# Moving the first attention head's weighted sum by one period, and turning the residual to tokens in squares of 32 and a trip through DRAM

## The chip, the cores and the metric

The kernel runs on one core of one Trainium2 chip. The metric is the device time of one execution in microseconds. A core has five engines with their own instruction streams: PE (TensorE, matrix products), DVE (VectorE), ACT (ScalarE), POOL (GpSimd) and SP (SyncE, which here only starts DMAs). They meet through semaphores. PE writes its products to PSUM, which has eight banks of 128 partitions x 2 KB; DVE and ACT read them from there.

## The reference

One layer of a hybrid block over 512 tokens and 16 meta tokens (T = 528), width 1024, all in fp32:

```python
h = h + 0.5 * swiglu(rmsnorm(h, ffn1_norm), w_gate, w_up, w_down)        # FFN 1, d_ff 2816
h = h + hybrid_mixer(rmsnorm(h, mix_norm), pos, k_top, w_in, w_ret_out, w_att_out, w_mix_out)
h = h + 0.5 * swiglu(rmsnorm(h, ffn2_norm), w_gate, w_up, w_down)        # FFN 2
y = rmsnorm(h, final_norm)                                               # the 512 real tokens

# in hybrid_mixer
merged = sigmoid(g_ret) * yr + sigmoid(g_att) * ya                       # retention and attention
return merged @ w_mix_out
```

`ya` is an attention of 8 heads of 128 over the keys that an index score selects (at most 128 of them here, and the 16 meta keys), with rotary positions: per head, scores of queries and keys, a softmax, and the sum of the values weighted by it.

## The kernel before, in words

*Layout and precision.* Activations are kept transposed: features on the 128 partitions, the 512 tokens along the free dimension, eight blocks of features. Every fp32 operand of a product is split in two parts, hi and lo (`split`: ACT copies hi, line L117, DVE subtracts, L118). A product is three matmuls per block, hi x hi, hi x lo and lo x hi (`mm3`, L157). Weights come in 1 MB or 512 KB loads on SP's queue (`raw`, two buffers) and are split into `whi` and `wlo` (three buffers each). A `Cols` object hands out one weight column block of 128 after the other; a product of one column with 512 tokens is 24 matmuls.

*Order.* PE's instructions stand in the order in which the program issues them; a few stretches also fix ACT and DVE. Elsewhere a scheduler orders the other engines' instructions. On every queue an instruction that waits holds up what stands behind it.

*PSUM in the mixer.* Two tiles of two banks (`mm_tile`) and four of one bank (`sm_tile`), each kind handed out in rotation. A tile is free again when its last reader is through.

*Attention heads* (loop over `h` in `range(AH)`, L2073 on). In head h's period PE does: the scores of head h (`psS`, 15 matmuls, L1970; DVE adds the bias and takes the maximum, L1973; ACT exponentiates, L1976); the query and key projections of head h+1 (`psaq`, `psak`), then rotated by ACT, DVE and POOL (L1292 to L1296) and split into `aq` and `ak`, which the next scores need; the weighted sum of head h-1 (`psao`); and a column of a gate projection (`psgate` or `psga`). For the weighted sum the probabilities have to lie with keys on the partitions. For heads 1 to 6 DVE transposes them in squares of 32 (`turn`, L1996), POOL writes them to DRAM (`pd`, L2000), SP reads them back in order (`land`, L2006), and `weigh_turned` multiplies them in the next period. For heads 0 and 7 PE transposes them (`transpose_p`, `psPT`, four blocks in four `sm` tiles), ACT and DVE split them from PSUM into `pth` and `ptl`, and `weigh_v` (`weighted`, L1537, L1538) multiplies them in the same period, behind one gate column for head 0 and head 7.

*The mixer's output* (L2133 on). Eight columns `psmo`, 24 matmuls each. Per column: ACT loads the residual `hc` from DRAM (`hd`); DVE adds the product to it (L2164); ACT scales it and splits it with DVE into `xh` and `xl` for FFN 2; ACT squares it, and POOL (DVE for the last column) adds up the squares (`ssum`, L296). The residual is also needed with tokens on the partitions, for the end of the kernel: `to_tokens` transposes two columns at a time on PE (eight transposes `psht`, L2149), and ACT copies them to `hTok` (four tiles of 128 tokens x 1024, L2151). The groups stand behind `psmo` of columns 2, 4 and 6, and, as `last_tokens`, behind the first gate product `psg` of FFN 2. Behind that comes the norm (`rstd_folded`): the sums of squares are folded (ACT L215, L218, DVE L217, L220), PE adds over partitions (`psn`, L225), DVE and POOL make the reciprocal root (L249, `rcol` L251, L276 to L282), PE spreads it (`psn`, L265).

*FFN 2* ends in products with tokens on the partitions. A first part of them is added into `hTok` in two bursts of four DVE additions (`add_sums`, L2241, 128x512 each), later parts likewise, and the final norm reads `hTok` (L2296).

Of the kernel before, what the change touches and what calls it, by code (L numbers as in the profile page):

```python
# [11 lines left out]
F32 = mybir.dt.float32  # L12
F32R = mybir.dt.float32r
AF = mybir.ActivationFunctionType
ALU = mybir.AluOpType
# [66 lines left out]
def kernel(ctx: ExitStack, tc: tile.TileContext, x, meta, g1, wg1, wu1, wd1, gm,  # L82
# [226 lines left out]
    gd = dpool.tile([2 * KD, P, S], F32, name="gd")  # L309

    pd = dpool.tile([2, S, 4, P], F32, name="pd")

    def gap(p, n):

# [1595 lines left out]
    with pool("ao") as ao:  # L1910
        vo = [ao.tile([P, AH, S], F32R, tag=f"vo{i}", name="vo") for i in range(2)]
        ao_parts = [(vo[0][:, c, :], vo[1][:, c, :]) for c in range(AH)]
        with pool("at") as at:
# [163 lines left out]
            for h in range(AH):  # L2077
                more = h + 1 < AH
                if h:
                    scores(q, k)  # L2080
                if more:
                    q, k = proj_q(w if h == 0 else None), proj_k()
                else:
                    wide_gate(sm_tile("psga"))
                    wide_gate()
                if pend is not None:
                    weigh_turned(h - 1, pend, vs[h - 1])
                    pend = None
                if h == 0:
                    with tc.manual_schedule(engines=BUSY):  # L2090
                        vs += split_values(raw, [v[:, 4:, :] for v in vo])
                    vrs.close()
                    crp = crs.enter_context(pool("cross", 1, side="right"))
                    cross = crp.tile([P, 16, 4, 32], F32, tag="cross", name="cross")
                    for j in range(3):
                        nc.gpsimd.memset(cross[:, 4 * j + 5 :, j, :], 0.0)
                if 0 < h and more:
                    turn(h)
                    wide_gate(sm_tile("psga"))
                    turned(h)  # L2100
                    pend = turned_parts()
                else:
                    pt = transpose_p()
                    wide_gate()
                    weigh_v(h, pt, vs[h])
                if h == 4:
                    place_tails(5)

        crs.close()

# [25 lines left out]
    hpool = ctx.enter_context(pool("hpool", 1))  # L2136
    hTok = [hpool.tile([P, D], F32, tag=f"hTok{b}", name=f"hTok{b}") for b in range(4)]
    ssum3 = hpool.tile([P, S], F32, tag="ssum3", name="ssum3")
    R3 = hpool.tile([P, S], F32, tag="R3", name="R3")
    new_ident2(hpool)  # L2140
    s2 = Sevens(S, S, wg2, wu2)
    s2.sums = ctx.enter_context(pool("sums2", 1))
    with pool("om") as ou:
        tp.update(pool=ou, bufs=3)
        def to_tokens(blocks):
            for c, hc in blocks:
                ps = sm_tile("psht")
                for b in range(4):
                    nc.tensor.transpose(ps[:, b * P : (b + 1) * P], hc[:, b * P : (b + 1) * P], ident)  # L2149
                for b in range(4):  # L2150
                    nc.scalar.activation(hTok[b][:, c * P : (c + 1) * P], ps[:, b * P : (b + 1) * P], AF.Copy)  # L2151

        cols = Cols(w_mo, 0, KD)
        pend = []
        for c in range(KD):
            hc = ou.tile([P, S], F32, tag="hc", name="hc", bufs=4)
            nc.scalar.dma_start(hc, hd[c])
            w = cols.next()
            ps = sm_tile("psmo")
            mm3([(ps, slice(0, S))], w, lambda k: mg[k], KD)  # L2160
            if len(pend) == 2:
                to_tokens(pend)
                pend = []
            nc.vector.tensor_tensor(hc, ps, hc, ALU.add)  # L2164
            h, l = new_x(c)
            if c % 4 == 0:
                s2.new_scaled()
            xc = s2.xn[c // 4][:, c % 4, :]
            nc.scalar.activation(xc, hc, AF.Identity, scale=gains[:, 2, c : c + 1])
            split(xc, h[:, :S], l[:, :S])  # L2170
            add_square(hc, ssum3, c == 0, ou, S, eng=(nc.gpsimd, nc.vector)[c == KD - 1])
            pend.append((c, hc))
        last_tokens = lambda a=pend: to_tokens(a)
        RS = slice(0, S)


        norm = rstd_folded(ssum3, D, R3, ou, lambda: mm_tile("psn"), lambda: sm_tile("psn"))
        raw0 = load_w(wg2[:, 0 : 2 * P], KD, 2 * P)
        ps0 = [sm_tile("psg") for _ in range(2)]
        for i in range(2):  # L2180
            w = split_w(raw0[:, :, i * P : (i + 1) * P])
            mm3([(ps0[i], RS)], w, xs, KD)
            if i == 0:
                last_tokens()
                next(norm)
        raw0 = load_w(wu2[:, 0 : 2 * P], KD, 2 * P)
        w = split_w(raw0[:, :, :P])
        for _ in norm:
            pass
    mgs.close()  # L2190
    accs.close()
    sel.close()
# [4 lines left out]
    with pool("hid2") as hidp, pool("f2ps", 8, PSUM) as f2ps, ExitStack() as later:  # L2197
# [39 lines left out]
            st.append(s2.gate_of(pss[1], ts[:, 1, :], R))  # L2237
            psus.append(tile_of(w, "psu"))

        def add_sums(b, cs, ps):  # L2240
            nc.vector.scalar_tensor_tensor(hTok[b][:, cs], ps, 0.5, hTok[b][:, cs], ALU.mult, ALU.add)  # L2241

        def products(parts, b, k, w, j, first, last):

# [6 lines left out]
        def down(f0, nf, n, taken_by):  # L2251


            d = {}
            steps = []
            for at in range(n):
                c, k0 = divmod(at * 2, nf)

                def pre(at=at, c=c, k0=k0):
                    if at % 2 == 0:  # L2260
                        d["raw"] = wpool.tile([P, 2048], F32, tag="raw", name="raw", bufs=2).rearrange("p (k c) -> p k c", k=4)
                    d[at] = d["raw"][:, at % 2 * 2 : at % 2 * 2 + 2]
                    rows = slice((f0 + k0) * P, (f0 + k0 + 2) * P)
                    nc.sync.dma_start(d[at], wd2[rows, c * S : (c + 1) * S].rearrange("(k p) c -> p k c", p=P))

                def run(w, lower, c=c, k0=k0):
                    if k0 == 0:
                        d["ps"] = [[(s2.bank("psd"), slice(0, S))] for _ in range(4)]
                        if f0 == groups[-1] and c == 1:
                            d["ps"][3] = [(s2.bank("psd")[:, : S // 2], slice(i * S // 2, (i + 1) * S // 2)) for i in range(2)]  # L2270
                    for b in range(4):
                        for k in range(k0, k0 + 2):
                            products(d["ps"][b], b, f0 + k, w, k - k0, k == 0, k == nf - 1)
                        if b == 1:
                            lower()
                            s2.catch_up()
                    if k0 == nf - 2:
                        for b in range(4):
                            add_sums(b, slice(c * S, (c + 1) * S), d["ps"][b][0][0])
                            taken_by(b, c)  # L2280
                    s2.next_sum4()

                steps.append((pre, lambda at=at: d[at], run))
            return steps, d
# [6 lines left out]
        def finish(b, c):  # L2291

            p, sums, hg = fin["p"], fin["sums"], fin["hg"]
            cs = slice(c * 512, (c + 1) * 512)
            junk = p.tile([P, 512], F32, tag="junk", name="junk", bufs=2)
            nc.scalar.activation(junk, hTok[b][:, cs], AF.Square, accum_out=sums[:, b, c : c + 1])  # L2296
            nc.vector.tensor_tensor(hg[b][:, cs], hTok[b][:, cs], fin["gfb"][:, cs], ALU.mult)
            if c == 0:
                nc.vector.tensor_scalar(sums[:, b, 0:1], sums[:, b, 0:1], 1.0 / D, EPS, ALU.mult, ALU.add)
                return None  # L2300
            ms = p.tile([P, 2], F32, tag="fms", name="fms", bufs=4)
            nc.vector.tensor_scalar(ms[:, 0:1], sums[:, b, 1:2], 1.0 / D, sums[:, b, 0:1], ALU.mult, ALU.add)
            nc.gpsimd.tensor_tensor(ms[:, 1:2], ms[:, 0:1], mhalf[:, 0:1], ALU.pow)
            return ms[:, 1:2]
# [54 lines left out]
        with tc.manual_schedule(engines=BUSY):  # L2359
# [5 lines left out]
                    products([part], 3, f0 + k, ws[k // 2 - 1], k % 2, False, k == 5)  # L2365
            ready = None
            for b in range(3):
                add_sums(b, slice(S, D), last["ps"][b][0][0])
                r = finish(b, 1)
                if ready:  # L2370
                    leave(*ready)
                ready = (b, r)
            sums, hg = fin["sums"], fin["hg"]
            for i, (ps, q) in enumerate(last["ps"][3]):
                cs = slice(S + q.start, S + q.stop)
                add_sums(3, cs, ps)
                junk = fp.tile([P, 512], F32, tag="junk", name="junk", bufs=2)
                nc.scalar.activation(junk[:, q], hTok[3][:, cs], AF.Square, accum_out=sums[:, 3, 1 + i : 2 + i])
                nc.vector.tensor_tensor(hg[3][:, cs], hTok[3][:, cs], fin["gfb"][:, cs], ALU.mult)
                if i == 0:  # L2380
                    nc.vector.tensor_scalar(sums[:, 3, 0:1], sums[:, 3, 1:2], 1.0 / D, sums[:, 3, 0:1], ALU.mult, ALU.add)
            leave(*ready)
# [31 lines left out]
```

## Time and profile before

| | |
|---|---|
| median of 3 runs | 1512.89 us (1512.02 to 1515.25) |
| the profiled execution | 1512.66 us, span 1510.8 us, mean granted clock 0.997 |
| PE busy | 1498.6 us, 99% of the span |
| DVE busy | 1113.5 us, 74% |
| ACT busy | 729.9 us, 48% |
| POOL busy | 122.2 us, 8% |
| mean DMA rate | 122 GB/s |

Head 0's sum begins at 910 us of the span and head 7's ends at 1068; the attention's output projection follows, the mixer's output fills 1111 to 1158, and FFN 2 the rest. A row of the timeline is: start, length, engine, line, operation, output<-inputs, shape, count, and in brackets how long the engine was idle before it and what ended that. The chain that ended last is the path that set the end; a row of it is start, length, engine, tile and line, count. PE's rows overlap a little, since matmuls are pipelined.

### The profile page before, as it was taken

What the parts mean: (1) busy time and instruction counts of PE and PEld (TensorE: products, weight loads), DVE (VectorE), ACT (ScalarE), POOL (GpSimd) and SP (SyncE); (2) the same over time, 40 slices, a digit from 0 to 9 for tenths busy, and PEclk for the clock granted to TensorE, in tenths of its full rate; (3) what the DMA queues carried; (4) which work ended last, traced back from release to release, by engine and by line L of the source; (5) the groups of instructions that cost most, each with busy time, mean ns of one, the idle gap of its engine ahead of it and who ended that gap; (6) DMA issues with size and microseconds to landing.
All of it is one profiled execution on the core that took longest, in us unless ns stands there. A gap on an engine that the chain in (4) does not pass through costs nothing.

```text
span 1510.8 us, 23879 instructions
## 1 busy us (share of the span) xinstructions
PE 1498.6 (99%) x9664; PEld 1361.2 (90%) x9664; DVE 1113.5 (74%) x1740; ACT 729.9 (48%) x1134; POOL 122.2 (8%) x169
## 2 busy tenths in 40 slices
PE   9999999999999999999999998999999999999998
PEld 8999999999988888888898887988888899899996
DVE  4988585786786768678978887787455888586675
ACT  5555263454354444443333356677345445254453
POOL 1000000002111120000000132331001000000000
PEclk9999999999999999999999999999999999999999
DMA  5232323226544444232322244566443223233232
GB/s 170 64 121 87 116 92 112 86 96 200 205 149 168 167 146 158 87 122 72 117 93 87 95 130 134 154 189 193 147 135 124 84 84 110 86 112 112 84 117 93
DMA packets 161918, 184.90 MB, mean 122 GB/s; under 512 B 12048, under 2 KB 130344, under 8 KB 161168
## 3 DMA queue, kind: packets, MB, share of 16 engines
q1 hardware_dynamic: 151056, 156.70, 32.3%
q0 software_dynamic: 5920, 17.68, 3.5%
q10 hardware_dynamic: 4832, 9.00, 1.7%
q8 instruction: 76, 1.25, 0.3%
q14 instruction: 34, 0.28, 0.1%
HBM read 161.05 MB, written 22.30 MB: 121 GB/s over the span
## 4 chain that ended last, share of the span: by engine, by line
PE 97%; DVE 1%; ACT 1%; issue 1%; DMA 0%; POOL 0%; POOLq 0%; DVEq 0%; ACTq 0%
PE psqX L157 14%; PE psd L157 8%; PE psd L2249 8%; PE psqY L157 7%; PE psrg L157 6%; PE psro L157 6%; PE psvX L1181 4%; PE psqZ L157 3%; PE psrk L157 3%; PE psu L157 3%; PE psrq L157 3%; PE psga L157 3%; PE psat L157 3%; PE psmo L157 3%; PE psak L157 3%; PE psaq L157 3%
## 5 line engine op out<-in xcount | busy, mean ns | idle before, releaser
L329 ACT ACTIVATE whi<-raw 128x1024 fp32r<-128x1024 f32 (+2 forms) x184 | 169.5, 924 | 129.0 <-PE psd L157 37.5
L330 DVE TENSOR_TENSOR wlo<-raw,whi 128x1024 fp32r<-128x1024 f32 (+2 forms) x184 | 198.6, 1083 | 40.6 <-ACT whi L329 40.5
L157 PE MATMUL psqX<-th,whi 128*128 128x264 f32 (+1 forms) x432 | 122.3, 283 | 0.0
L157 PE MATMUL psqX<-tl,whi 128*128 128x264 f32 (+1 forms) x432 | 122.3, 283 | 0.0
L157 PE MATMUL psqX<-th,wlo 128*128 128x264 f32 (+1 forms) x432 | 122.2, 283 | 0.0
L329 ACT ACTIVATE whi<-wsum 128x1024 fp32r<-128x1024 f32 x72 | 76.3, 1060 | 70.7 <-PE psd L2249 22.0
L117 ACT ACTIVATE whi<-raw 128x1024 fp32r<-128x1024 f32 (+1 forms) x60 | 62.2, 1043 | 86.0 <-PE psat L157 26.6
L330 DVE TENSOR_TENSOR wlo<-wsum,whi 128x1024 fp32r<-128x1024 f32 x72 | 87.8, 1221 | 12.5 <-ACT whi L329 12.5
L118 DVE TENSOR_TENSOR wlo<-raw,whi 128x1024 fp32r<-128x1024 f32 (+1 forms) x60 | 73.6, 1228 | 28.3 <-ACT whi L117 27.4
L157 PEld LDWEIGHTS psqX<-th,whi 128*128 128x128 f32 x432 | 82.1, 190 | 0.1
L157 PEld LDWEIGHTS psqX<-tl,whi 128*128 128x128 f32 x432 | 82.0, 190 | 0.0
L157 PEld LDWEIGHTS psqX<-th,wlo 128*128 128x128 f32 x432 | 82.0, 190 | 0.0
L157 PE MATMUL psro<-vo,whi 128*128 128x512 f32 x256 | 78.7, 389 | 0.0
L157 PE MATMUL psd<-hl,whi 128*128 128x264 f32 x352 | 71.3, 284 | 0.0
L157 PE MATMUL psd<-hh,wlo 128*128 128x264 f32 x352 | 70.8, 283 | 0.0
L157 PE MATMUL psd<-hh,whi 128*128 128x264 f32 x352 | 70.7, 282 | 0.0
L2249 PE MATMUL psd<-wlo,hh 128*128 128x512 f32 (+1 forms) x182 | 69.2, 382 | 0.0
L2249 PE MATMUL psd<-whi,hh 128*128 128x512 f32 (+1 forms) x182 | 69.2, 382 | 0.0
L2249 PE MATMUL psd<-whi,hl 128*128 128x512 f32 (+1 forms) x182 | 69.2, 382 | 0.0
L157 PEld LDWEIGHTS psro<-vo,whi 128*128 128x128 f32 x256 | 48.0, 188 | 10.1 <-DVE vo L330 0.2
L157 PEld LDWEIGHTS psd<-hh,wlo 128*128 128x128 f32 x352 | 54.5, 188 | 0.0
L157 PEld LDWEIGHTS psd<-hh,whi 128*128 128x128 f32 x352 | 54.2, 188 | 0.0
(476 smaller groups left out, 4540.8 us busy)
## 6 DMA issues: line engine op xcount, KB each, us to landing
raw<-in_ffn_w_up_dram SPq DMA_DIRECT2D x22, 1024.0 KB, 5.0
raw<-in_ffn_w_gate_dram SPq DMA_DIRECT2D x21, 1024.0 KB, 5.0
raw<-in_w_in_dram SPq DMA_DIRECT2D x18, 1024.0 KB, 5.0
raw<-in_w_in_dram SPq DMA_DIRECT2D x33, 512.0 KB, 3.8
raw<-in_ffn_w_down_dram SPq DMA_DIRECT2D x24, 512.0 KB, 4.4
w<-in_w_in_dram SPq DMA_DIRECT2D x24, 512.0 KB, 6.1
raw<-in_ffn_w_down_dram SPq DMA_DIRECT2D x12, 768.0 KB, 4.4
raw<-in_w_ret_out_dram SPq DMA_DIRECT2D x8, 1024.0 KB, 4.8
```

The source lines that it names most:

```text
L117: nc.scalar.activation(hi, src, AF.Copy)
L118: eng.tensor_tensor(lo, src, hi.bitcast(F32), ALU.subtract)
L157: nc.tensor.matmul(o, a[:, k, :], b[:, sl], start=first and k == 0 and i == 0, stop=last and k == nk - 1 and i == 2, skip_group_check=onto)
L329: nc.scalar.activation(hi, src, AF.Copy)
L330: return lambda: nc.vector.tensor_tensor(lo, src, hi.bitcast(F32), ALU.subtract)
L1181: nc.tensor.matmul(d[bank_][t], a, b[:, k, :], start=not onto and j + k + m == 0, stop=j + k == 3 and m == 2, skip_group_check=onto)
L2249: nc.tensor.matmul(ps, a[:, bs], m[:, j, cs], start=first and i == 0, stop=last and i == 2)
```

## The change

1. `weigh_v` of head 0 is issued in head 1's period, behind the projections for head 2, at the place where `weigh_turned` stands for the later heads. `pend` then always holds the parts of the head before; the sum of head 7 follows the loop.
2. `to_tokens` no longer uses PE, PSUM and ACT. Per column DVE transposes two halves of `hc` (128x256) in squares of 32 into `hTok`, which serves as staging. After every fourth column POOL writes the staged tiles to a DRAM tensor `hx` (eight DMAs of 128 KB each time, in runs of 512 bytes), and after the norm POOL reads `hx` back into `hTok` (four DMAs of 512 KB).
3. In `hx`, and so in `hTok`, the 512 features of a half stand in another order: the group of 32 within a block comes ahead of the block. The first addition of FFN 2 to each half of each tile (`in_order`) puts them right: four DVE operations of 128 elements a partition each, into a free tile (`spare`, or a half that has been read). `home` remembers where each half now is. Later additions are as before.

```diff
+    hx = dpool.tile([S, 2, 4, P], F32, name="hx")
...
                 if pend is not None:
-                    weigh_turned(h - 1, pend, vs[h - 1])
-                    pend = None
+                    (weigh_turned, weigh_v)[h == 1](h - 1, pend, vs[h - 1])
...
                 else:
-                    pt = transpose_p()
+                    pend = transpose_p()
                     wide_gate()
-                    weigh_v(h, pt, vs[h])
                 if h == 4:
                     place_tails(5)
+            weigh_v(AH - 1, pend, vs[AH - 1])
...
-        def to_tokens(blocks):
-            for c, hc in blocks:
-                ps = sm_tile("psht")
-                for b in range(4):
-                    nc.tensor.transpose(ps[:, b * P : (b + 1) * P], hc[:, b * P : (b + 1) * P], ident)
-                for b in range(4):
-                    nc.scalar.activation(hTok[b][:, c * P : (c + 1) * P], ps[:, b * P : (b + 1) * P], AF.Copy)
+        def to_tokens(c, hc):
+            half, j = divmod(c, 4)
+            for g in range(2):
+                t = hTok[2 * half + g]
+                nc.vector.transpose(t.rearrange("p (b j i) -> p b j i", j=4, i=32)[:, :, j, :],
+                                    hc[:, g * 2 * P : (g + 1) * 2 * P].rearrange("p (b i) -> p b i", i=32))
+                if j == 3:
+                    for a in range(4):
+                        nc.gpsimd.dma_start(hx[g * 2 * P : (g + 1) * 2 * P, half, a].rearrange("(b q) e -> q b e", q=32),
+                                            t[32 * a : 32 * a + 32].rearrange("p (b e) -> p b e", e=P))
...
-            if len(pend) == 2:
-                to_tokens(pend)
-                pend = []
...
-            pend.append((c, hc))
-        last_tokens = lambda a=pend: to_tokens(a)
+            if c < KD - 1:
+                to_tokens(c, hc)
...
             if i == 0:
-                last_tokens()
                 next(norm)
+                to_tokens(KD - 1, hc)
...
         for _ in norm:
             pass
+        for b in range(4):
+            nc.gpsimd.dma_start(hTok[b], hx[b * P : (b + 1) * P].rearrange("t h a e -> t (h a e)"))
...
-        def add_sums(b, cs, ps):
-            nc.vector.scalar_tensor_tensor(hTok[b][:, cs], ps, 0.5, hTok[b][:, cs], ALU.mult, ALU.add)
+        home, free = {}, [spare]
+
+        def in_order(b, c, ps):
+            t = hTok[b][:, c * S : (c + 1) * S]
+            o = home[b, c] = free.pop()
+            for a in range(4):
+                view = [x.rearrange("p (j a i) -> p a j i", a=4, i=32)[:, a] for x in (o, ps)]
+                nc.vector.scalar_tensor_tensor(view[0], view[1], 0.5, t[:, a * P : (a + 1) * P].rearrange("p (j i) -> p j i", i=32),
+                                               ALU.mult, ALU.add)
+            free.append(t)
+
+        def add_sums(b, c, ps, q=slice(0, S)):
+            if (b, c) not in home:
+                return in_order(b, c, ps)
+            t = home[b, c][:, q]
+            nc.vector.scalar_tensor_tensor(t, ps, 0.5, t, ALU.mult, ALU.add)
```

The remaining lines of the diff replace `hTok[b][:, cs]` by `home[b, c]` where the final norm reads it.

More of the change, by code (lines that the diff above doesn't have):

```diff
@@ L2138 @@
     ssum3 = hpool.tile([P, S], F32, tag="ssum3", name="ssum3")
+    spare = hpool.tile([P, S], F32, tag="spare", name="spare")
     R3 = hpool.tile([P, S], F32, tag="R3", name="R3")
@@ L2160 @@
             mm3([(ps, slice(0, S))], w, lambda k: mg[k], KD)
-            if len(pend) == 2:
-                to_tokens(pend)
-                pend = []
             nc.vector.tensor_tensor(hc, ps, hc, ALU.add)
@@ L2278, in run @@
                         for b in range(4):
-                            add_sums(b, slice(c * S, (c + 1) * S), d["ps"][b][0][0])
+                            add_sums(b, c, d["ps"][b][0][0])
                             taken_by(b, c)
@@ L2295, in finish @@
             junk = p.tile([P, 512], F32, tag="junk", name="junk", bufs=2)
-            nc.scalar.activation(junk, hTok[b][:, cs], AF.Square, accum_out=sums[:, b, c : c + 1])
-            nc.vector.tensor_tensor(hg[b][:, cs], hTok[b][:, cs], fin["gfb"][:, cs], ALU.mult)
+            nc.scalar.activation(junk, home[b, c], AF.Square, accum_out=sums[:, b, c : c + 1])
+            nc.vector.tensor_tensor(hg[b][:, cs], home[b, c], fin["gfb"][:, cs], ALU.mult)
             if c == 0:
@@ L2367 @@
             for b in range(3):
-                add_sums(b, slice(S, D), last["ps"][b][0][0])
+                add_sums(b, 1, last["ps"][b][0][0])
                 r = finish(b, 1)
@@ L2375 @@
                 cs = slice(S + q.start, S + q.stop)
-                add_sums(3, cs, ps)
+                add_sums(3, 1, ps, q)
                 junk = fp.tile([P, 512], F32, tag="junk", name="junk", bufs=2)
-                nc.scalar.activation(junk[:, q], hTok[3][:, cs], AF.Square, accum_out=sums[:, 3, 1 + i : 2 + i])
-                nc.vector.tensor_tensor(hg[3][:, cs], hTok[3][:, cs], fin["gfb"][:, cs], ALU.mult)
+                t = home[3, 1][:, q]
+                nc.scalar.activation(junk[:, q], t, AF.Square, accum_out=sums[:, 3, 1 + i : 2 + i])
+                nc.vector.tensor_tensor(hg[3][:, cs], t, fin["gfb"][:, cs], ALU.mult)
                 if i == 0:
```

## The prediction

> **What bounds the kernel now.** I read the chain that ended last first, then TensorE's own waits.
>
> ```profile
> PE 97%; DVE 1%; ACT 1%; issue 1%; DMA 0%; POOL 0%; POOLq 0%; DVEq 0%; ACTq 0%
> ```
>
> TensorE is 97% of the chain, so the change is worth what it takes off TensorE: instructions, waits or clock. TensorE's rows where head 0's weighted sum (psao) meets head 1's scores (psS), and the granted clock there (the eighth value of a window's row, after five busy times, 0.76 and 1.00) with a stretch of the next period below it:
>
> ```profile
> 910.49 0.40 PE L1537 MATMUL psao<-pth,vo 128*128 128x512 f32 x1
> ...
> 914.25 0.39 PE L1537 MATMUL psao<-ptl,vo 128*128 128x256 f32 x1 [1.85 <-DVE ptl L118]
> ...
> 914.62 3.00 PE L1970 MATMUL psS<-ak,aq 128*128 128x400 f32 x15
> ```
>
> ```profile
> 914.20:917.40 3.20, 3.15 (x18) 3.15 (x19) 1.90 (x9) 2.55 (x5) 0.95 (x1) 0.76 1.02 285
> 936.70:938.00 1.30, 0.41 (x2) 0.14 (x2) 1.21 (x2) 1.29 (x2) 0.00 (x0) 1.00 0.02 6
> ```
>
> The sum stands behind its transposes and one gate product only, and its last quarter waits 1.85 us for VectorE. Behind the wait the clock is 0.76. The chain prices it against the same work two heads later (start, length, count):
>
> ```profile
> 914.76 2.85 PE psS L1970 x15
> 917.61 6.31 PE psaq L157 x24
> ...
> 929.70 5.26 PE psgate L157 x23
> ...
> 951.29 2.26 PE psao L2028 x12
> 953.56 5.56 PE psga L157 x24
> 959.12 2.02 PE psS L1970 x15
> 961.14 5.47 PE psaq L157 x24
> ```
>
> The clock costs 2.85 - 2.02 on the scores and 6.31 - 5.47 on the query projection psaq: 0.83 + 0.84 = 1.67 us. With the wait, stall 1 is 1.85 + 1.67 = 3.52 us.
>
> Stall 2 is one head later. There only psgate (5.26) lies between the key projection psak and the next scores, which need the split keys ak:
>
> ```profile
> 934.98 1.06 ACT L117 ACTIVATE whi<-raw 128x1024 fp32r<-128x1024 f32 x1 [3.18 <-PE psgate L157]
> 935.95 0.63 ACT L117 ACTIVATE ak<-tmp 128x528 fp32r<-128x528 f32 x1
> ```
>
> ```profile
> 936.63 0.45 PE L1970 MATMUL psS<-ak,aq 128*128 128x400 f32 x1 [1.45 <-ACT ak L117]
> 937.97 2.10 PE L1970 MATMUL psS<-ak,aq 128*128 128x400 f32 x14 [0.89 <-DVE ak L118]
> ```
>
> 1.45 + 0.45 + 0.89 + 2.10 = 4.89 us for scores that take 2.02: stall 2 is 2.87 us, and the clock stayed at 1.00. From head 2 on psao (2.26) and psga (5.56) stand between, 7.82 us, and no wait is listed.
>
> **The change, part by part.** *Head 0's sum, one period later.* psao(0) goes between psak and psgate of head 1's period; TensorE issues the same instructions. Stall 1 goes as it stands: +3.52. For stall 2 the gap grows by psao's 2.26 to 5.26 + 2.26 = 7.5 us, and in the changed order ScalarE splits ak ahead of the whi that held it back here (that whi waits for psgate's end, and ak is queued behind it), as it does in later heads. ak was through on VectorE 0.9 + 0.45 + 1.45 = 2.8 us after psgate's end, 8.1 after psak's; without whi's 1.06 and without the wait for psgate it comes under 7.5. Stall 2 goes: +2.87. If ak stayed behind that whi, stall 2 would stay whole.
>
> What is late next: psaq now follows head 1's scores with nothing behind it to wait for, and it takes the PSUM bank of the fourth block of head 0's transposes, which is free when VectorE has read it (ptl, 256 wide).
>
> ```profile
> 911.50 2.36 DVE L118 TENSOR_TENSOR wlo<-raw,whi 128x1024 fp32r<-128x1024 f32 x2
> 913.78 0.42 DVE L118 TENSOR_TENSOR ptl<-psPT,pth 128x256 fp32r<-128x256 f32 x1
> 915.45 0.57 DVE L1973 CUSTOM_DVE_ANT_0 tmp<-psS,bias 128x400 f32<-128x400 f32 x1 [1.26 <-PE psS L1970]
> ```
>
> In the changed order one wlo and the bias sum L1973 stand ahead of it in place of two wlo: 911.50 + 2.36 / 2 + 0.5 (0.57 less its overlap) = 913.2, and with 0.42 the bank is free at 913.6. Scores that begin at 910.49 end at 912.5. A new stall of 1.1 us: -1.1. Its ends are 0 (the read comes earlier) and 3.52 (as long as the old one, clock and all); I take 1.1 without a clock loss, since of the two gaps shown it is nearer to 1.45, which left 1.00.
>
> The Trainium skill, "TensorE: Matmul & The Clock Gate", section "Why this matters for your kernels", gives gaps of over about 3 us as what drops the clock to half. The trace disagrees for stall 1: after a gap of 1.85 us it shows 0.76. By the page the 1.67 us would have another cause and stay, and the whole sum below would be 5.9 instead of 7.6.
>
> SP's queue keeps its loads, but the lands of the turned probabilities move by one head against the weight loads (raw): from head 1 on four lands stand ahead of three raws. The old queue has that order from the next head on, where no wait follows; taken at 0, priced in the rivals.
>
> *Tokens by VectorE.* Gone are 32 transposes on TensorE, in four groups (psht), and 32 copies on ScalarE, which is not on the chain. Three groups stood alone between psmo's columns:
>
> ```profile
> 1127.72 0.87 PE psht L2149 x8
> ...
> 1157.61 5.44 PE psg L157 x24
> 1163.05 0.87 PE psht L2149 x8
> 1163.92 0.34 PE psn L225 x4
> ```
>
> 3 x 0.87 = +2.61. The fourth, behind psg(0), gave VectorE time as well: psn needs the folded sum of squares (L220).
>
> ```profile
> 1157.64 0.69 DVE L2164 TENSOR_TENSOR hc<-psmo,hc 128x512 f32<-128x512 f32 x1 [1.06 <-PE psmo L157]
> 1158.51 1.23 DVE L118 TENSOR_TENSOR wlo<-raw,whi 128x1024 fp32r<-128x1024 f32 x1 [0.18 <-ACT whi L117]
> 1159.72 0.69 DVE L296 TENSOR_TENSOR ssum<-ssum,sq 128x512 f32<-128x512 f32 x1
> ...
> 1162.49 0.68 DVE L220 TENSOR_TENSOR tmp<-ssum,tmp 64x512 fp32r<-64x512 f32 x1 [0.70 <-ACT tmp L218]
> ```
>
> ```profile
> L1996 DVE STREAM_TRANSPOSE cross<-pj x24: 323/545/714, 919.1 to 1034.4; 128x416 f32<-128x416 f32 x6, 128x288 f32<-128x288 f32 x6, 128x160 f32<-128x160 f32 x6, 128x512 f32<-128x512 f32 x6
> ```
>
> ```profile
> L2000 POOL DMA_DIRECT2D pd<-cross x24: 648/672/707, 922.8 to 1039.9; - x24
> ```
>
> From ssum's start to L220's end are 1163.17 - 1159.72 = 3.45 us. In the changed order two transposes of 128x256 follow the last hc (between 0.32 for 160 elements and 0.71 for 512: 0.43 each, some 0.37 apart), then wlo, xl (as long as ssum), and only then ssum: 1158.25 + 0.75 + 1.14 + 0.62 = 1160.75, so L220 ends at 1164.2. psg(0) now ends at 1163.05, and psn starts at about 1164.2 instead of 1163.92: a wait of 1.15 us and a term of -0.3. Its ends are +0.87 (L220 keeps its time) and -0.3 - 1.67 (the gap drops the clock); taken -0.3, again by the 1.45 gap.
>
> The other fourteen transposes lie beside psmo: per column VectorE has hc, wlo, xl and now 0.86 more, 0.69 + 1.23 + 0.69 + 0.86 = 3.5 of some 5.4 us (psg's length, the same product); without that cover at most 0.86 a column. Of the DMAs, sixteen writes and four reads go to POOL's queue, at pd's 0.67 each 13 us in all. ssum of column 4 is queued behind the first eight writes, 5.4 us, which is a column; ScalarE's next square waits for it, and has the next column's time. rcol, on the way to the norm, is behind four of the last eight: 1159 + 4 x 0.67 = 1161.7, before its input exists. Behind rcol stand four writes and the reads, through by about 1170; even with 10 us of landing they are in long before the first use:
>
> ```profile
> 1211.38 1.88 DVE L2241 SCALAR_TENSOR_TENSOR hTok<-psd,hTok 128x512 f32<-128x512 f32 x3
> ...
> 1227.53 0.42 DVE L545 TENSOR_TENSOR g<-psqZ,p 128x256 f32<-128x256 f32 x1 [0.58 <-PE psqZ L157]
> ```
>
> ```profile
> 1200.00:1226.00 26.00, 26.00 (x123) 21.80 (x122) 21.25 (x34) 11.41 (x20) 0.00 (x0) 1.00 0.25 81
> ```
>
> Eight of these adds become four each, of 128 elements. 512 take 0.69 (the slowest of three in 1.88 overlap), 256 elements of another VectorE operation 0.42, so 128 some 0.28: four make 1.1, +0.45 an add, +1.8 for each burst of four. VectorE is idle 26 - 21.25 = 4.75 us in that stretch and TensorE waits for nothing; after the second burst VectorE itself waits for TensorE (0.58). Taken at 0; uncovered, 2 x 1.8 = 3.6.
>
> **Sum.** 3.52 + 2.87 - 1.1 + 2.61 - 0.3 = 7.6 us. The profiled execution took 1512.66, 0.2 under the median of the runs shown (1512.89): 1505.1, say 1505.
>
> **The rivals.** *The new waits drop the clock.* Both new gaps, 1.1 and 1.15 us, cost 1.67 more, and the first adds another half: 7.6 - 3.3 - 0.9 = 3.4, 1509. For it: 1.85 us were enough. Against: 1.45 and then 0.89 were not. With only one of them the time is 1506.7, within the forecast's own range. The same 1506.7 comes out if stall 1's slow stretch has another cause than the wait and stays (7.6 - 1.67 = 5.9; 0.05 of the chances, counted with the forecast; against it speaks that 0.76 stands right behind the wait). That is what the Trainium skill's page on the clock gate would make of it.
>
> *Nothing measurable comes of it.* The stalls of the attention only move: psaq's wait takes the place of psao's at the full 3.52, stall 2 goes, the groups go (+2.61), psn's wait drops the clock (-2.0), and the adds in FFN 2 come out uncovered (-3.6): 0.1, so 1512.5. For it: VectorE is behind in each of these places. Against: the worked-out slack in three of them, and 4.75 us idle in the last.
>
> *Slower: the weight loads stand behind the lands.* A land waits on SP for POOL's write, and three raws wait behind it. If TensorE then waits in each of heads 1 to 6 as long as in stall 1, that is 6 x 1.85 = 11.1 against 7.6, 1516.2, and with its clock loss 6 x 3.52 = 21, 1526. It decides from 7.6 / 6 = 1.3 us a head. For it: head 1's period loses the raw that stood ahead of its lands. Against: later heads run that order without a wait.
>
> **How the numbers follow.** Forecast with its own range 1502 to 1508: 0.64 (low end: neither new stall, 7.6 + 1.1 + 1.17 = 9.9; high end: one clock loss and half of one burst). New waits with clock: 0.16, 1508 to 1510. Nothing measurable: 0.08. Slower: 0.12. A measurement of this kernel tells 0.2%, 3 us, from no change. Faster by more is the forecast and nearly all of the first rival: 0.79; within: 0.09; slower: 0.12. The range is 1502 to 1511: it leaves out the slower case and part of the third.
>
> **What would show it.** Right: no wait of psao, none of psS on ak; one wait of psaq on ptl near 912.5, about 1.1 us, with the clock at 1.00 behind it; psmo columns end to end; one wait of psn on L220 of about 1.2 us; no wait of psd on the adds. Wrong: a clock under 0.9 behind either wait, waits of psaq, psak or psga on whi in heads 2 to 6, a wait of psmo on hc, or the reads of hTok landing after 1200.

## The result, and the profile after

The changed kernel takes 1506.18 us (median of 5 runs, 1505.79 to 1506.70); the kernel before, run beside it, 1512.55 (1511.53 to 1515.25). The ratio is 0.9957, 95% interval 0.9943 to 0.9970: 6.4 us faster, against 7.6 forecast (1505, range 1502 to 1511). The profiled execution spans 1504.7 us, 6.1 less than that of before.

TensorE's waits in the changed kernel (total, times, longest):

```profile
PE psg L655 <- DVE idle L623: 1.5, 1, 1.5
PE psn L225 <- DVE tmp L220: 1.2, 1, 1.2
PE psaq L157 <- DVE stat L1975: 0.6, 1, 0.6
PE psS L1972 <- DVE ptl L118: 0.2, 1, 0.2
```

The first stands at the kernel's start and was there before. The waits of psao on ptl and of psS on ak are gone, and three shorter ones are new. The chain through the heads (line numbers are 2 higher than before):

```profile
914.30 5.73 PE psaq L157 x24
920.03 5.77 PE psak L157 x48
925.80 1.98 PE psao L1539 x12
927.80 5.58 PE psgate L157 x24
933.37 2.02 PE psS L1972 x15
935.39 5.47 PE psaq L157 x24
```

psao(0) stands between psak and psgate, and the next scores follow without a gap. TensorE's timeline at head 1's scores and at the norm:

```profile
911.09 0.71 PE L1972 MATMUL psS<-ak,aq 128*128 128x400 f32 x3
912.01 1.73 PE L1972 MATMUL psS<-ak,aq 128*128 128x272 f32 x12 [0.21 <-DVE ptl L118]
914.30 0.50 PE L157 MATMUL psaq<-xh,whi 128*128 128x512 f32 x1 [0.56 <-DVE stat L1975]
...
1156.91 0.61 PE L225 MATMUL psn<-ones_r,tmp 128*128 128x2 f32 x4 [1.24 <-DVE tmp L220]
```

Between them the eight columns of psmo are one piece of the chain:

```profile
1106.71 43.53 PE psmo L157 x192
```

Where the time went is read from the start of the same TensorE instruction in both profiles:

| instruction | before | after | apart | step |
|---|---|---|---|---|
| first psak of head 1's projections | 897.70 | 898.29 | +0.59 | |
| first psaq of head 2's period | 939.91 | 935.23 | -4.68 | -5.27 |
| first psg | 1157.44 | 1150.07 | -7.37 | -2.69 |
| psn, L225 | 1163.68 | 1156.91 | -6.77 | +0.60 |
| last psd | 1503.94 | 1497.18 | -6.76 | +0.01 |
| end of the span | 1510.8 | 1504.7 | -6.1 | +0.6 |

The attention gave 5.27 (forecast 5.3), the groups between psmo's columns 2.69 (2.61). The norm cost 0.60 (0.3). FFN 2 neither gave nor took anything. Two steps were not in the sum: 0.59 ahead of the change and 0.6 behind the last matmul.

### The profile page after: what moved, and what is told of

It reads as the page before. It is cut to its first block, busy times and chain, and to the rows that moved or that the text cites. A ratio compares the mean times of both kernels' runs of the same rounds, so it can differ in the third digit from the quotient of the medians.

```text
span 1504.7 us, 23856 instructions
## 1 busy us (share of the span) xinstructions
PE 1493.9 (99%) x9632; PEld 1356.3 (90%) x9632; DVE 1121.6 (75%) x1780; ACT 724.0 (48%) x1102; POOL 136.0 (9%) x189
## 4 chain that ended last, share of the span: by engine, by line
PE 96%; DVE 1%; ACT 1%; issue 1%; DMA 0%; POOL 0%; POOLq 0%; ACTq 0%; DVEq 0%
PE psqX L157 14%; PE psd L157 8%; PE psd L2270 8%; PE psqY L157 7%; PE psrg L157 6%; PE psro L157 6%; PE psvX L1183 4%; PE psqZ L157 3%; PE psrk L157 3%; PE psu L157 3%; PE psrq L157 3%; PE psga L157 3%; PE psat L157 3%; PE psmo L157 3%; PE psak L157 3%; PE psaq L157 3%
```

## The experiments

Four kernels separate the parts, four measure the norm's wait and the clock, and three follow what was left.

**Each part alone.** `head_only` is the kernel before with point 1 of the change, `tokens_only` with points 2 and 3.

```diff
# head_only, against the kernel before
-                    weigh_turned(h - 1, pend, vs[h - 1])
-                    pend = None
+                    (weigh_turned, weigh_v)[h == 1](h - 1, pend, vs[h - 1])
...
-                    pt = transpose_p()
+                    pend = transpose_p()
                     wide_gate()
-                    weigh_v(h, pt, vs[h])
...
+            weigh_v(AH - 1, pend, vs[AH - 1])
```

> The kernel before with head 0's weighted sum moved by one period, and nothing else. By the prediction's working stalls 1 and 2 go (3.5 and 2.9 us) and a new wait of psaq, with its neighbours, costs 1.1 to 1.2: about 5.2 us under the kernel before, ratio 0.9966; psht stays in four groups of 0.87. Rival (the gain in the changed kernel comes mostly from the transposes, the stalls only move): under 3 us.

Measured: 1507.79 us, ratio 0.9961 (0.9948 to 0.9975): 5.9 us by the ratio, 5.2 between the medians. Its psS waits on ak and its psao on ptl are gone, and psaq waits 0.6 on L1973's read, as in the changed kernel. The rival falls.

> The kernel before with the residual turned by VectorE and DRAM, and head 0's sum where it was. Three groups of 0.87 go, and the sum over partitions (psn) comes 0.6 later as in the changed kernel, where it waits 1.24 us: about 2.0 us under the kernel before, ratio 0.9987. Stalls 1 and 2 stand as before, the granted clock behind stall 1 again at 0.6 to 0.8. Rival (the sixteen writes, four reads and the additions in pieces cost something that the changed kernel's other gain hides): no gain, or slower.

Measured: 1511.55 us, ratio 0.9989 (0.9980 to 0.9999): 1.7 us by the ratio, 1.5 between the medians. The gain is there, so the additions in pieces and the DMAs hide no loss of that size. 0.0039 and 0.0011 add up to 0.0050, and the two parts together gave 0.0043 (0.0030 to 0.0057): within the intervals that is no different from two parts that act apart from each other. One point of the expectation is wrong. Stall 1 is as long as before, but the clock does not fall behind it; it falls behind stall 2:

```profile
915.32 0.39 PE L1539 MATMUL psao<-ptl,vo 128*128 128x256 f32 x1 [1.93 <-DVE ptl L118]
915.54 0.28 PE L1539 MATMUL psao<-pth,vo 128*128 128x256 f32 x1
915.65 0.17 PE L1540 MATMUL psao<-ptail,vtail 80*128 80x16 f32 x1
915.68 2.26 PE L1972 MATMUL psS<-ak,aq 128*128 128x400 f32 x15
...
937.46 2.72 PE L1972 MATMUL psS<-ak,aq 128*128 128x400 f32 x14 [0.89 <-DVE ak L118]
939.98 0.63 PE L157 MATMUL psaq<-xh,whi 128*128 128x512 f32 x1
```

The same in windows (the granted clock is the eighth value of a row):

```profile
915.70:917.70 2.00, 2.00 (x18) 2.00 (x17) 1.19 (x5) 1.79 (x2) 0.52 (x1) 1.00 1.04 288
...
939.50:941.50 2.00, 2.00 (x8) 1.71 (x7) 1.24 (x7) 1.54 (x7) 0.00 (x0) 0.50 1.09 379
```

**Stall 1 shortened where it stood.** The first of two kernels that issue the second half of the value splits behind head 0's transposes, so that VectorE reads the fourth block one wlo earlier; the sum is not moved.

```diff
# before_values_late, against the kernel before
                 if h == 0:
+                    pt = transpose_p()
                     with tc.manual_schedule(engines=BUSY):
                         vs += split_values(raw, [v[:, 4:, :] for v in vo])
...
-                    pt = transpose_p()
+                    if h:
+                        pt = transpose_p()
                     wide_gate()
```

> The kernel before with one edit: the second half of the value splits is issued behind head 0's transposes instead of ahead of them, so that ptl 256 is read one wlo earlier, at about 912.3 in place of 914.2. The sum stays in its own period. If the wait of 1.85 us is what drops the clock, both go: wait under 0.4 us, clock 1.00 behind it, 1.6 + 1.67 = 3.2 us under the kernel before, ratio 0.9979; stall 2 stays at 2.9. If the slow stretch has another cause it stays, and the gain is 1.6 us, ratio 0.9989.

Measured: 1510.31 us, ratio 0.9982 (0.9972 to 0.9991). In its profile psao has no wait, the clock behind it is 1.00 (by itself that would show little, since it is 1.00 behind stall 1 in `tokens_only` as well; what decides is worked out below), the first psak of head 1's period comes 3.57 us earlier than in the kernel before, counted from the first psak of head 0's, and stall 2 is as it was:

```profile
911.96 0.41 DVE L118 TENSOR_TENSOR ptl<-psPT,pth 128x256 fp32r<-128x256 f32 x1
```

```profile
913.00:915.00 2.00, 2.00 (x16) 2.00 (x16) 2.00 (x3) 1.97 (x4) 1.19 (x1) 1.00 0.13 20
```

So an edit that only turns round the order of two pieces of work gets half of the attention's gain. Its ten runs lie in two groups, 1509.22 to 1509.56 and 1511.06 to 1512.01, with medians 1.8 apart, which is what one fall of the clock behind stall 2 would make. The mean granted clock of the runs goes with it: 0.999 in all five of the first group, 0.997 or 0.998 in all five of the second. The profile is of the first group, so where the second loses its clock stays an inference.

> The changed kernel with the same edit. The waits of head 1's scores on ptl (0.21) and of psaq on the fourth bank (0.56) should go, so that scores and the change to psaq take 2.0 us in place of 3.2: 1.2 us under the changed kernel, ratio to the kernel before 0.9950. Rival (wlo, now behind the values, is late in the bank's place): psaq or psak waits on wlo for 0.5 us or more and the time is the changed kernel's.

This is the same edit in the changed kernel. Measured: 1505.44 us, ratio 0.9947 (0.9930 to 0.9965). Against the profile of the changed kernel TensorE's last matmul comes 1.20 earlier. The two short waits are gone:

```profile
910.92 2.18 PE L1972 MATMUL psS<-ak,aq 128*128 128x400 f32 x15
912.94 0.43 PE L157 MATMUL psaq<-xh,whi 128*128 128x512 f32 x1
```

**The norm's wait, taken away.** VectorE's order in the last column of psmo is written out: the wlo for the up projection goes behind the norm, ssum comes ahead of xl.

```diff
# norm_first, against the changed kernel (added lines; what they replace is left out)
+            if c == KD - 1:
+                break
...
+        ws = [split_w(raw0[:, :, i * P : (i + 1) * P]) for i in range(2)]
+        with tc.manual_schedule(engines={mybir.EngineType.DVE}):
+            nc.vector.tensor_tensor(hc, ps, hc, ALU.add)
+            to_tokens(KD - 1, hc)
+            h, l = new_x(c)
+            xc = s2.xn[c // 4][:, c % 4, :]
+            nc.scalar.activation(xc, hc, AF.Identity, scale=gains[:, 2, c : c + 1])
+            add_square(hc, ssum3, False, ou, S, eng=nc.vector)
+            split(xc, h[:, :S], l[:, :S])
+            mm3([(ps0[0], RS)], ws[0], xs, KD)
+            next(norm)
+            raw0 = load_w(wu2[:, 0 : 2 * P], KD, 2 * P)
+            w = split_w(raw0[:, :, :P])
+        mm3([(ps0[1], RS)], ws[1], xs, KD)
```

> The changed kernel with VectorE's order in the last column of psmo written out: hc, the two transposes, ssum, xl, L217, L220, and only then the wlo for the up projection. The transposes then fill the time in which ssum waits for ScalarE's square (ready 2.0 us after psmo's end), and L220 ends 5.4 us after psmo's end in place of 6.6. The wait of psn falls from 1.24 to 0.2 or less: 1.0 to 1.2 us under the changed kernel, ratio to the kernel before about 0.9950. Rival (the two wlo that now stand behind it delay the spread of the norm or psu): the time moves to a wait of psn (L265) or psu and nothing is gained.

Measured: 1505.51 us, ratio 0.9947 (0.9932 to 0.9963). VectorE in the changed kernel and then in this one:

```profile
1150.99 0.77 DVE L2153 STREAM_TRANSPOSE hTok<-hc 128x256 f32<-128x256 f32 x2
1151.69 1.18 DVE L118 TENSOR_TENSOR wlo<-raw,whi 128x1024 fp32r<-128x1024 f32 x1
1152.79 0.69 DVE L118 TENSOR_TENSOR xl<-wsum,xh 128x512 fp32r<-128x512 f32 x1
1153.40 0.69 DVE L296 TENSOR_TENSOR ssum<-ssum,sq 128x512 f32<-128x512 f32 x1
```

```profile
1151.19 0.77 DVE L2153 STREAM_TRANSPOSE hTok<-hc 128x256 f32<-128x256 f32 x2
1152.54 0.69 DVE L296 TENSOR_TENSOR ssum<-ssum,sq 128x512 f32<-128x512 f32 x1 [0.58 <-ACT sq L295]
```

```profile
PE psn L225 <- DVE tmp L220: 0.2, 1, 0.2
```

ssum begins 2.28 us after psg's first matmul, as in the kernel before (1159.72 - 1157.44); in the changed kernel it was 3.33 (1153.40 - 1150.07). The two transposes still stand ahead of it, but with wlo and xl out of the way they lie in the time in which ssum waits for ScalarE's square. So in this order the transposes cost nothing, and what made psn late was that wlo and xl stood ahead of ssum as well.

**Both edits together** (`best`).

> The changed kernel with both edits, the values split behind the transposes and VectorE's order in the last column. If the two act apart from each other, 1.0 + 1.1 = 2.1 us under the changed kernel, about 1504.2, ratio to the kernel before 0.9943.

Measured: 1504.39 us, ratio 0.9941 (0.9928 to 0.9953). Of the waits only the start's and psn's 0.2 are left, and the last matmul comes 2.38 earlier than in the changed kernel.

**The norm's wait, made longer.** L220 is done once or twice more.

```diff
# fold_1 (fold_2: range(2)), against the changed kernel
         for _ in folded(ssum, f, tmp()[:, :S]):
             pass
+        for _ in range(1):
+            nc.vector.tensor_tensor(f[64:P], ssum[:64, :S], f[:64].bitcast(F32), ALU.subtract)
```

> The changed kernel with L220 done twice (the same values written again): psn's wait grows from 1.24 by 0.62 to 1.86 us, the length of stall 1. If a wait of this length is enough to drop the clock, the granted clock behind it falls under 0.8 for some 4 us and the cost is 0.6 + 1.7 = 2.3 us against the changed kernel; if length alone is not what decided at stall 1, the clock stays at 1.00 and the cost is 0.6.

> The changed kernel with L220 done three times, a wlo between the second and the third: psn's wait grows to 1.24 + 0.62 + 1.14 + 0.62 = 3.6 us. Both the reading of stall 1 and a rule of about 3 us have the clock fall here: 2.4 + 1.7 = 4.1 us against the changed kernel; without a fall 2.4.

Measured: 1507.73 us (ratio 0.9962, 0.9947 to 0.9976) and 1510.95 us (0.9985, 0.9975 to 0.9995). Against the changed kernel's profile, from psg's first matmul on, `fold_1` lost 2.4 us and `fold_2` 5.8. TensorE's row (L234 is the added line) and the clock behind it, for `fold_1`:

```profile
1156.81 0.58 PE L225 MATMUL psn<-ones_r,tmp 128*128 128x2 f32 x4 [2.04 <-DVE tmp L234]
```

```profile
1156.80:1158.00 1.20, 1.19 (x7) 1.10 (x8) 1.19 (x2) 0.00 (x0) 0.00 (x0) 1.00 0.00 0
1158.00:1159.00 1.00, 1.00 (x5) 0.73 (x4) 0.00 (x0) 0.00 (x0) 0.93 (x1) 0.71 0.02 4
1159.00:1160.00 1.00, 1.00 (x4) 0.81 (x3) 0.76 (x4) 0.00 (x0) 1.00 (x3) 0.50 0.64 132
```

and for `fold_2`:

```profile
1159.49 0.98 PE L225 MATMUL psn<-ones_r,tmp 128*128 128x2 f32 x4 [4.02 <-DVE tmp L234]
```

```profile
1159.50:1160.50 1.00, 1.00 (x5) 1.00 (x6) 0.00 (x0) 0.00 (x0) 0.00 (x0) 0.50 0.69 111
...
1164.00:1166.00 2.00, 2.00 (x6) 1.55 (x5) 0.00 (x0) 0.00 (x0) 0.52 (x2) 0.51 0.85 205
```

Behind the wait of 2.04 us the clock goes to half, as the first of the two readings expects, though only more than 1 us after TensorE has gone on. After 4.02 us it is at half at once and stays there for 6.8 us, so that this execution of `fold_2` cost 1.7 more than expected. Both profiles are of the longer runs of their kernels (1508.03 of 1507.04 to 1508.19, 1512.14 of 1510.35 to 1512.41). By ratios and medians `fold_1` cost 0.8 to 1.6 us against the changed kernel (2.3 expected with a fall, 0.6 without) and `fold_2` 4.2 to 4.8 (4.1 expected), so what the two profiles show need not have happened in every run.

**The kernel before, looked at again, and the end of the span.** `before_again` is the kernel before without an edit. `before_pool20` is the kernel before with twenty more DMAs on POOL's queue, a copy of parts of hTok that nothing reads:

```diff
# before_pool20, against the kernel before
+    hx = dpool.tile([20, P, 256], F32, name="hx")
...
         for _ in norm:
             pass
+        for i in range(20):
+            nc.gpsimd.dma_start(hx[i], hTok[i % 4][:, :256])
```

> The kernel before, unchanged, for another profile: the end 6.6 us after the last matmul, stall 1 of 1.85 and stall 2 of 1.45 and 0.89 us. If the length of a wait decided on the clock, it falls behind stall 1 again and stays behind stall 2; if it is a matter of when a wait begins, it may be the other way.

> The kernel before with twenty DMAs of 128 KB added on POOL's queue behind the norm of FFN 2, which copy parts of hTok to a DRAM tensor that nothing reads (extra work, outputs as they were). In the four kernels looked at with the turn through DRAM the span ends 7.2 us after TensorE's last matmul, in the three without it 6.6. If DMAs added on POOL's queue bring these 0.6 us, they show here as well: 7.2. If not, 6.6, and the cause lies elsewhere in that part of the change. It is also another look at stalls 1 and 2: the clock may fall behind stall 1 (as in the kernel before), behind stall 2 (as with the tokens alone), behind both or neither; each fall costs about 1.6.

Single runs: 1513.21 and 1516.01 us. From the end of the last matmul to the end of the span it is 6.6 us in the first and 7.2 in the second; it is 6.6 to 6.7 in the other three profiles without the turn through DRAM, and 7.2 to 7.3 in the seven with it on POOL's queue. So the DMAs added on POOL's queue, with the DRAM tensor that they write, bring the 0.6 us at the end without the rest of the change. What the chip does in that time has no row. The scores behind the two stalls, `before_again` first, then `before_pool20` (from the chain):

```profile
915.25 2.11 PE psS L1970 x15
...
936.88 3.43 PE psS L1970 x14
```

```profile
916.23 3.33 PE psS L1972 x15
...
939.08 3.54 PE psS L1972 x14
```

With full clock these are 2.11 (as in the first) and 2.10 (as in the kernel before). The clock fell behind stall 2 in the first, and behind both stalls in the second.

**The DMAs on SP's queue** (`best_sp`: `best` with `nc.sync` for `nc.gpsimd` in the sixteen writes and four reads of hx).

> The changed kernel with both edits, and its sixteen writes and four reads of hx on SP's queue in place of POOL's. If it is DMAs on POOL's queue that cost 0.6 us at the end, that is gained: about 1503.6, ratio to the kernel before 0.9937. Against it: the weight loads of FFN 2 then stand on SP behind writes and reads that wait for each other, and a late raw would show as a wait on whi; from 0.6 us of such a wait on nothing is gained.

Measured: 1503.92 us, ratio 0.9935 (0.9918 to 0.9951), the fastest of all. The end after the last matmul is 6.8 us, and there is no wait on whi. Of the 0.6 us it regains 0.4, which therefore go with the queue; the other 0.2 come with the DMAs on either queue, or with the DRAM tensor, which no run tells apart. Whether the kernel is truly faster than `best` the intervals don't tell.

## Why the prediction was right

*Head 0's sum.* Both stalls went, for the reasons given: psao's operands are ready a period later, and ak is split ahead of whi and under cover of psao and psgate. 5.27 of 5.3.

*The new wait of psaq* was 0.21 + 0.56, and from the scores' start to psaq it took 914.30 - 911.09 = 3.21 us against 3.1 worked out. But the bank named for it was wrong. psaq begins at 914.30, when L1975's read of the first scores has ended, and that is before ptl 256 ends:

```profile
914.16 0.08 DVE L1975 DVE_READ_ACCUMULATOR2_ANT stat<- 128x1 f32 x1
914.16 0.42 DVE L118 TENSOR_TENSOR ptl<-psPT,pth 128x256 fp32r<-128x256 f32 x1
```

So psaq took a bank that becomes free with the first scores, not that of the fourth block. (In `values_late`, where the fourth block is read earlier, psaq begins at 912.94, before the first scores are read: which bank it gets is not fixed by the order of the tiles.) The size came out because both reads follow the same wlo.

*Stall 1's clock.* The sum was right, its place was chance. The prediction read one execution, in which the clock fell behind stall 1 and not behind stall 2, as a rule of lengths: "of the two gaps shown it is nearer to 1.45, which left 1.00". Five profiles of kernels with both stalls, or with stall 2 alone, show that the same waits go either way: of four waits of 1.85 to 1.93 two had the clock fall, and of five of 1.45 + 0.89 three. Of the four profiles with both stalls three show one fall, at one place or the other, and one shows two, so 1.67 was a fair term (1.58, if the scores are set against the same scores at full clock, 2.11 in `before_again`, and not against the 2.02 of a later head). Waits of 1.24 and less (psn, psaq) left it at 1.00 in every profile, so the two new waits were rightly taken without a fall. The rival in which they drop the clock did not come.

What decides is in the same traces. The clock goes to half for 3.41 us at a time (6.83 in `fold_2`). Within one execution two falls begin a whole multiple of that time apart: 23.89 us in `before_pool20` (7 x 3.413), 590.51 between the fall of the kernel before and the one that every profile has behind the last matmul (173 x 3.413). So the execution is cut into periods of 3.41 us whose place has nothing to do with the waits. Rows of single periods, each counted from the fall behind the last matmul (the value behind the comma is TensorE's busy time); the first two are of the kernel before at stall 1, the next of `before_again`, the last two of `tokens_only`, there too at stall 1:

```profile
912.43:915.84 3.41, 1.59 (x11) 1.59 (x12) 2.15 (x4) 2.36 (x4) 1.28 (x1) 1.00 0.61 169
915.84:919.25 3.41, 3.41 (x14) 3.02 (x13) 3.07 (x17) 2.93 (x8) 0.00 (x0) 0.50 0.51 139
...
913.29:916.71 3.42, 1.98 (x14) 1.98 (x15) 2.16 (x5) 2.36 (x4) 1.28 (x1) 1.00 0.69 179
...
911.34:914.76 3.42, 2.05 (x11) 1.52 (x9) 3.36 (x6) 3.39 (x5) 0.74 (x3) 1.00 0.00 0
914.76:918.17 3.41, 2.85 (x20) 2.81 (x21) 2.16 (x9) 2.35 (x4) 1.28 (x1) 1.00 0.93 249
```

In the kernel before, nearly the whole wait lies in one period, TensorE is idle for 1.82 us of it, and the next period runs at half. In the other two a period's edge divides the wait; TensorE is idle for at most 1.44 us of one period, and the clock stays. Between 20 us and the last matmul the thirteen profiles have fifteen periods with more than 1 us idle: the seven with 1.77 us or more are followed by a fall, the eight with 1.46 or less are not. So the limit lies between these two, at about half a period, and whether a wait of 1.85 us reaches it depends on where the period's edge falls. The new waits, 0.77 and 1.24 us, can't reach it wherever it falls: to take them without a fall was right, but not because they are near to 1.45. The two parts of stall 2, 2.34 us in all, can. Why `fold_2` stays at half for a second period, ahead of which TensorE was idle for only 0.36 us, no run shows.

*The rule of about 3 us* in the Trainium skill's page "TensorE: Matmul & The Clock Gate" gave 1506.7, and the median is 1506.2, but not for that reason: the slow stretch went with the wait, in `before_values_late` too, and falls came after waits of 1.85, 1.92 and 2.04 us. That page's section "Part 1: The HAM clock gate (the "warmup" mystery)" also says that the clock is either full or half and that the activity window runs freely, so that it depends on the phase when a change comes. The trace agrees with both: 0.50 in whole periods of the fall, and equal waits with and without one, by the place of the period's edge.

*The groups.* 2.69 for 2.61; psmo is one piece.

*The norm* is the term that was mis-sized: 0.60 lost in place of 0.3. L220 ended 6.79 us after psg's start, 6.76 worked out. The slip was in what it was set against: 1163.92 is psn's place on the chain, which counts a matmul from the end of the one before it; its start in the timeline was 1163.68, and 1164.2 less that is 0.5.

*The additions in FFN 2* were 0.28 us each as estimated (273 to 293 ns), VectorE's busy time in that stretch of work (1200 to 1226 before, 1193.2 to 1219.2 in the changed kernel, which is there 6.8 us ahead) rose from 21.25 to 22.58 of 26 us, and TensorE waited for none of it. The reads of hTok were issued by 1167.7, some 37 us ahead of the first addition at 1204.6.

*Slower by the weight loads behind the lands* did not come: no wait on whi in any head. The rival in which nothing measurable comes of it did not come either; its sum is -0.1, not 0.1 (2.87 + 2.61 - 2.0 - 3.6), which changes nothing in the forecast.

*Outside the sum.* The 0.6 us at the end belong to the change, 0.4 of them through POOL's queue, and no step of the prediction looked behind the last matmul. The 0.59 ahead of it do not: the first psaq of head 0 starts between 891.9 and 893.3 us in the profiles of kernels whose code up to there is the same.

## What to carry to other kernels

A wait at one place of the chain is often an order of work on another engine: the largest single wait here went with two pieces of VectorE's work turned round, and the norm's with one wlo put behind it, while the engine's load stayed the same. When work moves to another engine, look at what it stands ahead of there: the transposes and an xl came ahead of ssum, and the norm's first matmul came 0.60 us later. The old group of transposes on TensorE had hidden little of the norm, since L220 ended 0.1 us behind psg (1163.17 against 1163.05). And price a stall from several executions where the clock is part of it, since the same wait can cost 1.6 us more or nothing more, by where it lies in the periods of 3.41 us.

## What the runs showed that was not expected

The clock fell in some executions after a wait of 1.85 to 2.04 us and not in others (1.92 and 1.93): it goes to half for a period of 3.41 us when TensorE was idle for 1.77 us or more of the period before, and not after 1.46 or less, whether that is one wait or two. A fall costs 1.5 to 1.7 us; the one of 6.83 us after the wait of 4.02 cost about 3. Twenty DMAs more on POOL's queue, some 340 us before the end, made the span end 0.6 us later behind the last matmul (7.2 against 6.6), whether the rest of the change was there or not.
